# Memory keys copied out of PSUM unscaled and scaled in SBUF, diagonals of 1/rms on ScalarE, later sums of squares, and another branch's gates first

## The chip, the cores and the metric

The kernel runs on one core of one Trainium2 chip. The metric is the time of one execution in microseconds (us), as the median of several runs; smaller is better. In what follows PE is TensorE (the matmul engine), DVE is VectorE, ACT is ScalarE, POOL is GpSimd, and SP is the engine that issues most DMAs.

## What is computed

One step of a one-layer decoder with three parallel branches, for a prompt of 512 tokens and 8 samples of 8 tokens (T = 576 columns in all, 1024 features), with a memory of 256 tokens. Only the part at the program's start and the gates at its end are touched by the change:

```python
def _rmsnorm(x, g):
    y = xf * lax.rsqrt(jnp.mean(xf * xf, axis=-1, keepdims=True) + NORM_EPS)
    return (y * g.astype(jnp.float32)).astype(x.dtype)

def _mem_kv(mem, norm_g, w_kv):
    kv = _rmsnorm(mem, norm_g) @ w_kv           # memory keys and values: outputs, used again later
    mk, mv = jnp.split(kv, 2, axis=-1)

xn = _rmsnorm(x, norm_g)
proj = xn @ w_in                                # one projection that feeds every branch
merged = (sigmoid(m_conv) * (y_conv @ w_branch[0])     # branch 0
          + sigmoid(m_rwkv) * (y_rwkv @ w_branch[1])   # branch 1
          + sigmoid(m_mem)  * (y_mem  @ w_branch[2]))  # branch 2
out = _rmsnorm_final(x + merged @ w_out)
```

## The kernel before

**Number format.** Every operand of a large matmul is split into a high and a low part (`wh` and `wl` of a weight `w`, `mh` and `ml` of the memory, `xh` and `xl` of the normed input), and each product is three matmuls: high by high, high by low, low by high. A weight comes in halves of 128x512 (256 KB each): ACT rounds the half to `wh`, and POOL or DVE subtracts to get `wl` (in the first stage they take turns, half by half).

**Order.** The order on PE is written out by hand. A main generator yields after every few matmuls (one tick), and at each tick every "lane" (a queue of side generators) takes a step; a side generator that yields a number n sleeps for n ticks. So a lag such as `MLAG` sets after how many ticks a side chain's next matmul is put into PE's order. On DVE, ACT, POOL and SP a scheduler decides the order, and each of these engines works its own list strictly from top to bottom: an instruction that waits holds up all that stand behind it.

**The first stage** (`kv`, up to about 68 us) computes memory keys and values:
- Eight key tiles j = 0 to 7 (`w_mk`), each 24 matmuls of 256 columns and 16 ticks. Two tiles share one PSUM buffer `m`, and there are two such buffers, so a tile's buffer must have been read before the second tile pair after it can start.
- Then the values (`w_mv`), 8 steps k of 12 matmuls of 512 columns and 4 ticks each, into two PSUM buffers that are filled alternately, and read at the end into `vst` by ACT.
- The memory is not normed before the product. `mem_rms` computes 1/rms of each memory token beside it (`inv_rms`): ACT squares, DVE adds up to `sq`, PE sums over partitions (line 169, into `z`), DVE makes `ss`, POOL takes the power to `rs`, a diagonal matrix `dg` is made from `rs`, and PE multiplies a matrix of ones by it (line 189), which broadcasts 1/rms over the partitions (`bcs`). `kout` then multiplies each key tile in PSUM by `bcs` on DVE, into `kst`, and every four tiles a DMA on ACT's queue writes `o_mk`.
- The input x (`tr`, four DMAs between key tiles) goes through the same `inv_rms`, in `norm_x`; its broadcast stays in PSUM (`c` and `o`), and for each of 8 feature tiles DVE makes `xn` (two instructions, one per half of the columns), ACT rounds it to `xh` and DVE subtracts to `xl`.
- `mem_rms` and `norm_x` queue one behind the other in the same lane.

**After it** come the projection tiles by `w_in` (48 matmuls of 288 columns each, the first of them is the lora tile), the three branches, and the output product. Weight buffers of this stage are three deep, so the fourth half's `wh` waits until PE has used the first. While PE waits for the rwkv branch's chains, some sigmoid gates are computed ahead (`early_gates`), in the order of `EARLY`, and parked in DRAM; `branch` loads a gate that is there and computes one that isn't. Seven gates get done that way. Branch 2 runs before branch 1, and during branch 1 `wout` prepares the output weights, one step per `lag` ticks.

Of the kernel before, what the change touches and what calls it, by code (L numbers as in the profile page):

```python
# [12 lines left out]
ALU = mybir.AluOpType  # L13
# [8 lines left out]
XS = (2, 3, 5, 6)  # L22
AH = 3
LK = 1
XL2 = 4
MLAG = 51
XLAG = 19


CB = 2  # L30
# [55 lines left out]
def hybrid_step(ctx, tc, x_nat, x_t, mem_t, w_in, w_br, w_mk, w_mv, w_o, kc, vc, swkv,  # L86
# [3 lines left out]
    V, S, G, TE, DMA = (nc.vector, nc.scalar, nc.gpsimd, nc.tensor, nc.sync)  # L90

    def tt(e, out, a, b, op):
        e.tensor_tensor(out=out, in0=a, in1=b, op=op)  # L93
# [4 lines left out]
    def act(out, in_, f=AF.Copy, **k):  # L98
        S.activation(out, in_, f, **k)  # L99
# [22 lines left out]
    def pc(n, j):  # L122
        a = PCOL[n][0] + j
        return par[:, a:a + 1]
# [5 lines left out]
    ident = idt  # L130
# [24 lines left out]
    def inv_rms(tr, ntok, half, pool, ones, lags, out):  # L155
        nt = (ntok + 127) // 128
        sq = pool.tile([128, ntok], F32, name="sq")
        for k in range(8):
            t = pool.tile([128, ntok], F32, name="xn", bufs=2)
            act(sq if k == 0 else t, tr[k], AF.Square)  # L160
            if k:
                tt(V, sq, sq, t, ALU.add)
        yield lags[0]
        z = psd.tile([128, 512], F32, name="s")
        ss = pool.tile([128, nt], F32, name="ss")
        rs = pool.tile([128, nt], F32, name="rs%d" % nt)
        for i in range(nt):
            n = min(128, ntok - i * 128)
            TE.matmul(z[0:n, i:i + 1], sq[:, i * 128:i * 128 + n], ones[:, 0:1], start=True, stop=True)
        nf = ntok // 128  # L170
        for q in (slice(0, nf), slice(nf, nt))[:1 + (nt > nf)]:
            n = 128 if q.start == 0 else ntok - nf * 128
            V.tensor_scalar(ss[0:n, q], z[0:n, q], 1.0 / 1024, 1e-6, op0=ALU.mult, op1=ALU.add)
            tt(G, rs[0:n, q], ss[0:n, q], nhalf[0:n, q], ALU.pow)
        dgs = []
        for i in range(nt):
            n = min(128, ntok - i * 128)
            dg = pool.tile([128, 128], F32, name="dg%d" % i)
            V.tensor_scalar(dg[0:n], ident[0:n], rs[0:n, i:i + 1], None, op0=ALU.mult)
            dgs.append(dg)  # L180
        yield lags[1]
        bc = [pch.tile([128, 512], F32, name=n) for n in "co"[:ntok // half]]
        for i in range(nt):
            n = min(128, ntok - i * 128)
            t0 = i * 128
            while t0 < i * 128 + n:
                h = t0 // half
                t1 = min(i * 128 + n, (h + 1) * half)
                TE.matmul(bc[h][:, t0 - h * half:t1 - h * half], ones[0:n],
                          dgs[i][0:n, t0 - i * 128:t1 - i * 128], start=True, stop=True)  # L190
                t0 = t1
        out += [rs, bc]
# [82 lines left out]
    chain_lane, post_lane, prep_lane, inv_lane, mrg_lane = (Lane() for _ in range(5))  # L275
# [10 lines left out]
    with tc.tile_pool(name="xi", bufs=1) as xi:  # L286
        mtr = xi.tile([128, 8, 256], F32, name="mtr")
        trs = [keep.tile([128, 2, T], F32, name="tr", tag=t) for t in SLOTS]
        tr = [trs[k // 2][:, k % 2, :] for k in range(8)]
        ones = xi.tile([128, 128], F32, name="ones")  # L290
        V.memset(ones, 1.0)
        mh = xi.tile([128, 8, 256], F32R, name="mh")
        ml = xi.tile([128, 8, 256], F32R, name="ml")


        def mem():
            for k in range(8):
                g = pc("norm_mem", k)
                act(mh[:, k, :], mtr[:, k, :], scale=g)
                stt(ml[:, k, :], mtr[:, k, :], g, mh[:, k, :].bitcast(F32), ALU.mult, ALU.subtract)  # L300

        mrs, xrs = [], []
        kst = keep.tile([128, 8, 256], F32, name="kst", tag="s4")
        bcs = xi.tile([128, 256], F32, name="bcs")

        def mem_rms():
            yield from inv_rms([mtr[:, k, :] for k in range(8)], 256, 256, xi, ones, (MLAG, 8), mrs)
            act(bcs, mrs[1][0][:, 0:256])

        def norm_x():  # L310
            yield from inv_rms(tr, T, HT, xi, ones, (XLAG, XL2), xrs)
            for k in range(8):
                xn = xi.tile([128, T], F32, name="xn", bufs=2)
                for h in range(2):
                    stt(v3(xn)[:, h], v3(tr[k])[:, h], pc("norm_in", k), xrs[1][h][:, 0:HT], ALU.mult, ALU.mult)
                act(xh[:, k, :], xn)
                tt(V, xl[:, k, :], xn, xh[:, k, :].bitcast(F32), ALU.subtract)

        def kout(j, ps):
            while not mrs:  # L320
                yield 0
            tt(V, kst[:, j, :], ps[:, j % 2, 0:256], bcs, ALU.mult)
            if j % 4 == 3:
                S.dma_start(out=o_mk[j - 3:j + 1].rearrange("j p m -> p j m"), in_=kst[:, j - 3:j + 1, :])

        def ahead(n):
            if n < 8:
                nxt.append(wload(w_mk[n].rearrange("p k f -> p (k f)"), xi, KBUF))
            elif n < 16:
                nxt.append(wload(w_mv[n - 8], xi, KBUF))  # L330

        nxt = []

        def load_x(j):
            for i in range(4):
                if XS[i] == j:
                    DMA.dma_start(out=trs[i], in_=x_t[:, 2 * i:2 * i + 2])
                    if i == 3:
                        prep_lane.q.append(norm_x())

        def kv():

            z = psd.tile([128, 512], F32, name="s")
            for _ in range(WARM):
                TE.matmul(z[:, 0:128], ones, ones, start=True, stop=True)
            DMA.dma_start(out=mtr[:, 0], in_=mem_t[:, 0])
            ahead(0)
            for a, b in ((1, 2), (2, 4), (4, 6), (6, 8)):
                DMA.dma_start(out=mtr[:, a:b], in_=mem_t[:, a:b])
            DMA.dma_start(out=idt, in_=const_d[:, 0:128])  # L350
            for i in range(1, AH):
                ahead(i)
            mem()
            prep_lane.q.append(mem_rms())
            for j in range(8):
                if j % 2 == 0:
                    ps = pm.tile([128, 2, 512], F32, name="m")
                ahead(j + AH)
                yield from mm(None, mh, ml, 256, ps[:, j % 2:j % 2 + 1], nxt.pop(0))
                post_lane.q.append(kout(j, ps))  # L360
                load_x(j)
            pv = [pm.tile([128, 2, 512], F32, name="m") for _ in range(2)]
            for k in range(8):
                ahead(8 + k + AH)
                load_x(8 + k)
                parts = nxt.pop(0)
                if k == LK:
                    lora_weights(xi)
                    DMA.dma_start(out=con[:, 0:NX], in_=const_d[:, 128:NC1])
                    DMA.dma_start(out=shp, in_=sshift)  # L370
                    DMA.dma_start(out=scv, in_=sconv)
                for q in range(4):
                    t, n = (q // 2, q % 2) if k == 7 else (q % 2, q // 2)
                    h, l = parts[n]
                    ts = slice(t * 128, t * 128 + 128)
                    for i, (a, b) in enumerate(((mh, h), (mh, l), (ml, h))):
                        TE.matmul(pv[t][:, n, :], a[:, k, ts], b,
                                  start=(k == 0 and i == 0), stop=(k == 7 and i == 2))
                    yield
            for t in range(2):  # L380
                st = xi.tile([128, 1024], F32, name="vst")
                act(st.rearrange("p (n f) -> p n f", n=2), pv[t], scale=mrs[0][:, t:t + 1])
                S.dma_start(out=o_mv[t * 128:t * 128 + 128, :], in_=st)
        lo_eng[:] = [G, V]
        drive(kv())
        while prep_lane.busy():
            prep_lane.step()
        lo_eng[:] = [G]


# [9 lines left out]
    def etile(tag, dt=F32, **k):  # L400
        return el.tile([128, T], dt, name="e" + tag, tag=tag, **k)

    EARLY = [(i, j) for i in (1, 2) for j in range(8)]
    gates = {}
    QT = ("r", "k", "A", "B", "C", "D", "E1", "F")
    qt = []
# [9 lines left out]
    with ExitStack() as rctx:  # L416
# [81 lines left out]
        def early_gates():  # L498
            for i, j in EARLY:
                ps = yield from mm(w_in[WM[i] + j])  # L500
# [756 lines left out]
            yield lag  # L1257


    prep_lane.q.append(wout(0, 27))  # L1260
    drive(branch(1, *parts, merged=(mgh, mgl)))
    for _ in wout(1, 0):
        pass
# [8 lines left out]
    for hf in range(2):  # L1272
        h, l = wo[hf]
        for i in range(5):
            n = 128 if i < 4 else 64
# [4 lines left out]
            for q, (c0, c1) in enumerate(((0, 256), (256, 512)) if last else ((0, 512),)):  # L1280
                ps = pm.tile([128, 2, 512], F32, name="m")
# [121 lines left out]
```

## Time and profile before

| | |
|---|---|
| median of 3 runs | 1235.23 us (1234.74 to 1237.84) |
| the profiled execution | 1235.45 us, its span 1233.6 us |
| PE busy | 1186.9 us, 96% of the span |
| DVE, ACT, POOL busy | 48%, 43%, 47% |
| mean granted clock of PE | 0.994 |

PE is the engine that nearly always works, so the time is what PE has to do plus what it waits. Its waits are few: the first 70 us, the rwkv stage from 92 to 630 us, and the last 5 us. A clock of 1.00 is 2.4 GHz, one of 0.50 is 1.2 GHz.

### The profile page before, as it was taken

What the parts mean: (1) busy time and instruction counts of PE and PEld (TensorE: products, weight loads), DVE (VectorE), ACT (ScalarE), POOL (GpSimd) and SP (SyncE); (2) the same over time, 40 slices, a digit from 0 to 9 for tenths busy, and PEclk for the clock granted to TensorE, in tenths of its full rate; (3) what the DMA queues carried; (4) which work ended last, traced back from release to release, by engine and by line L of the source; (5) the groups of instructions that cost most, each with busy time, mean ns of one, the idle gap of its engine ahead of it and who ended that gap; (6) DMA issues with size and microseconds to landing.
All of it is one profiled execution on the core that took longest, in us unless ns stands there. A gap on an engine that the chain in (4) does not pass through costs nothing. (4 is left out here: it accounts for less than half of the span.)

```text
span 1233.6 us, 25594 instructions
## 1 busy us (share of the span) xinstructions
PE 1186.9 (96%) x10158; PEld 1100.8 (89%) x10158; DVE 587.0 (48%) x1514; ACT 524.9 (43%) x1120; POOL 573.8 (47%) x521
## 2 busy tenths in 40 slices
PE   7999979999899999999989999999999999999997
PEld 7798979989798988988879898889899999999976
DVE  7856866468675686647673315213113100134233
ACT  6563446435463544546344435333233222233222
POOL 4535532555535465454543545333334454446642
PEclk9999989999999999999999999999999999999999
DMA  8642222132321322222322225653632222225522
GB/s 290 213 126 72 70 72 63 59 91 58 91 65 53 89 68 84 90 86 70 110 80 74 69 71 171 195 181 123 208 97 87 80 84 86 78 86 161 161 105 78
DMA packets 93056, 129.39 MB, mean 105 GB/s; under 512 B 36988, under 2 KB 41320, under 8 KB 92936
## 3 DMA queue, kind: packets, MB, share of 16 engines
q1 hardware_dynamic: 55888, 110.20, 28.3%
q10 hardware_dynamic: 37048, 17.56, 5.4%
q8 instruction: 80, 1.31, 0.5%
q14 instruction: 40, 0.33, 0.1%
HBM read 115.96 MB, written 11.47 MB: 103 GB/s over the span
## 5 line engine op out<-in xcount | busy, mean ns | idle before, releaser
L93 POOL TENSOR_TENSOR wl<-w,wh 128x512 fp32r<-128x512 f32 x274 | 366.5, 1340 | 490.0 <-ACT wh L99 451.4
L245 PE MATMUL m<-xh,wh 128*128 128x288 f32 x1680 | 370.4, 302 | 0.5 <-ACT vst L99 0.5
L245 PE MATMUL m<-xl,wh 128*128 128x288 f32 x1680 | 369.4, 301 | 0.0
L245 PE MATMUL m<-xh,wl 128*128 128x288 f32 x1680 | 365.2, 299 | 0.0
L99 ACT ACTIVATE wh<-w 128x512 fp32r<-128x512 f32 x290 | 180.5, 627 | 294.2 <-PE m L245 169.1
L245 PEld LDWEIGHTS m<-xh,wh 128*128 128x128 f32 x1680 | 268.8, 189 | 8.6 <-issue 3.7
L245 PEld LDWEIGHTS m<-xl,wh 128*128 128x128 f32 x1680 | 269.2, 189 | 6.4 <-issue 2.9
L245 PEld LDWEIGHTS m<-xh,wl 128*128 128x128 f32 x1680 | 269.4, 189 | 3.0 <-issue 2.1
L96 DVE SCALAR_TENSOR_TENSOR ev<-ev,m 128x576 f32<-128x576 f32 x32 | 24.2, 755 | 168.4 <-PE m L245 110.3
L245 PE MATMUL m<-yh,wh 128*128 128x288 f32 x384 | 82.9, 297 | 0.0
L245 PE MATMUL m<-yh,wl 128*128 128x288 f32 x384 | 82.8, 297 | 0.0
L245 PE MATMUL m<-yl,wh 128*128 128x288 f32 x384 | 82.8, 297 | 0.0
L245 PEld LDWEIGHTS m<-yh,wl 128*128 128x128 f32 x384 | 61.7, 188 | 2.1 <-issue 2.1
L245 PEld LDWEIGHTS m<-yl,wh 128*128 128x128 f32 x384 | 61.7, 188 | 2.1 <-issue 2.1
L245 PEld LDWEIGHTS m<-yh,wh 128*128 128x128 f32 x384 | 61.7, 189 | 2.1 <-issue 2.1
L93 DVE TENSOR_TENSOR c<-c,tmp 108x84 f32<-108x84 f32 (+23 forms) x248 | 56.6, 228 | 5.4
L93 DVE TENSOR_TENSOR tmp<-c,nin 108x84 f32<-108x84 f32 (+23 forms) x248 | 54.8, 221 | 6.7 <-issue 1.2
L96 DVE SCALAR_TENSOR_TENSOR sb<-o,pcl,sb 64x64 f32<-64x64 f32 x112 | 31.6, 282 | 52.1 <-PE o L887 46.0
L99 ACT ACTIVATE osb<-o 64x128 f32<-64x128 f32 x72 | 19.7, 274 | 52.3 <-DVE sb L96 30.5
L93 DVE TENSOR_TENSOR vu<-o,vu 64x128 f32<-64x128 f32 x56 | 15.9, 284 | 46.6 <-PE o L869 45.6
L99 ACT ACTIVATE E<-m,par 128x32 f32<-128x32 f32 (+1 forms) x75 | 27.2, 418 | 22.2 <-PE m L245 14.1
L99 ACT ACTIVATE sb<-sb,pcl 128x128 f32<-128x128 f32 x56 | 22.5, 401 | 29.4 <-DVE sb L96 18.8
(441 smaller groups left out, 1796.2 us busy)
## 6 DMA issues: line engine op xcount, KB each, us to landing
w<-w_in_in SPq DMA_DIRECT2D x210, 256.0 KB
w<-w_br_in SPq DMA_DIRECT2D x48, 256.0 KB
kb<-kc_in SPq DMA_DIRECT2D x16, 512.0 KB
kb<-vc_in SPq DMA_DIRECT2D x16, 512.0 KB
w<-w_mk_in SPq DMA_DIRECT2D x16, 256.0 KB
w<-w_mv_in SPq DMA_DIRECT2D x16, 256.0 KB
w<-w_o_in SPq DMA_DIRECT2D x16, 256.0 KB
nin<-scr ACTq DMA_DIRECT2D x24, 144.0 KB
```

Of the source, the lines that this page charges most:

```text
L93: e.tensor_tensor(out=out, in0=a, in1=b, op=op)
L96: V.scalar_tensor_tensor(out=out, in0=a, scalar=s, in1=b, op0=op0, op1=op1)
L99: S.activation(out, in_, f, **k)
L245: TE.matmul(ps[:, hf, :n], a[:, f], b[:, k, hf * n:hf * n + n], start=(k == 0 and i == 0), stop=(k == 7 and i == 2))
```

## The change

Five edits. `MLAG`, `XLAG` and `XL2` are larger, so the sums of squares and the broadcast of the memory and of x are asked of PE later. The diagonals `dg` are made by ACT instead of DVE. A key tile leaves PSUM as it is, by an ACT copy, and POOL multiplies four tiles at a time by `bcs` in SBUF. `mem_rms` has a lane of its own. And `EARLY` begins with the gates of branch 2 instead of branch 1 (the `lag` of `wout` then depends on how many gates of branch 1 are left; with 9 or more matmul tiles it is 27 as before).

```diff
-XL2 = 4
-MLAG = 51
-XLAG = 19
+XL2 = 5
+MLAG = 90
+XLAG = 42
...
             dg = pool.tile([128, 128], F32, name="dg%d" % i)
-            V.tensor_scalar(dg[0:n], ident[0:n], rs[0:n, i:i + 1], None, op0=ALU.mult)
+            act(dg[0:n], ident[0:n], scale=rs[0:n, i:i + 1])
...
         def mem_rms():
             yield from inv_rms([mtr[:, k, :] for k in range(8)], 256, 256, xi, ones, (MLAG, 8), mrs)
             act(bcs, mrs[1][0][:, 0:256])
+
+            for j in range(0, 8, 4):
+                while kdone[0] < j + 4:
+                    yield 0
+                tt(G, kst[:, j:j + 4, :], kst[:, j:j + 4, :], bcs.unsqueeze(1).to_broadcast([128, 4, 256]), ALU.mult)
+                S.dma_start(out=o_mk[j:j + 4].rearrange("j p m -> p j m"), in_=kst[:, j:j + 4, :])
...
-        def kout(j, ps):
-            while not mrs:
-                yield 0
-            tt(V, kst[:, j, :], ps[:, j % 2, 0:256], bcs, ALU.mult)
-            if j % 4 == 3:
-                S.dma_start(out=o_mk[j - 3:j + 1].rearrange("j p m -> p j m"), in_=kst[:, j - 3:j + 1, :])
...
-            prep_lane.q.append(mem_rms())
+            inv_lane.q.append(mem_rms())
...
                 yield from mm(None, mh, ml, 256, ps[:, j % 2:j % 2 + 1], nxt.pop(0))
-                post_lane.q.append(kout(j, ps))
+                act(kst[:, j, :], ps[:, j % 2, 0:256])
+                kdone[0] = j + 1
...
-    EARLY = [(i, j) for i in (1, 2) for j in range(8)]
+    EARLY = [(i, j) for i in (2, 1) for j in range(8)]
...
-    prep_lane.q.append(wout(0, 27))
+    nt = 16 - sum((1, j) in gates for j in range(8))
+    prep_lane.q.append(wout(0, min(27, (24 * nt - 16) // 8 - 1)))
```

Where the edits move instructions, at three places. First, DVE in the key stage, before the change (the number behind a name tells buffers apart; `ss_340` is the memory's sum of squares, which its 1/rms needs, and `wl_291` belongs to the second half of key tile 5):

```order
L93 TENSOR_TENSOR wl_254<-w_251,wh_253 128x512
L93 TENSOR_TENSOR wl_291<-w_288,wh_290 128x512
L173 TENSOR_SCALAR ss_340<-s_339 128x2
L179 TENSOR_SCALAR dg0_346<-idt_77,rs2_341 128x128
L179 TENSOR_SCALAR dg1_348<-idt_77,rs2_341 128x128
L93 TENSOR_TENSOR sq_505<-sq_505,xn_508 128x576
```

and the same place now (`wl_407` is the second half of value step k = 0, `wl_457` that of step k = 1):

```order
L93 TENSOR_TENSOR wl_255<-w_252,wh_254 128x512
L93 TENSOR_TENSOR wl_293<-w_290,wh_292 128x512
L93 TENSOR_TENSOR wl_331<-w_328,wh_330 128x512
L93 TENSOR_TENSOR wl_370<-w_367,wh_369 128x512
L93 TENSOR_TENSOR wl_407<-w_404,wh_406 128x512
L93 TENSOR_TENSOR wl_457<-w_454,wh_456 128x512
L173 TENSOR_SCALAR ss_429<-s_428 128x2
L93 TENSOR_TENSOR sq_506<-sq_506,xn_509 128x576
```

The memory's `ss` has moved behind four more weight halves; on PE its matmul (line 169) stands after 18 matmuls of key tile 5 instead of 8 of tile 3, and the broadcast (line 189) after 8 matmuls of tile 6.

Second, ACT from there to the last key tile, now (`kst` from `m_360` are key tiles 4 and 5, from `m_447` tiles 6 and 7; `dg0_435` and `dg1_437` are the memory's diagonals; before, no `kst` and no `dg` stood on ACT):

```order
L99 ACTIVATE dg1_437<-idt_77,rs2_430 128x128
L99 ACTIVATE kst_111<-m_360 128x256
L99 ACTIVATE wh_494<-w_492 128x512
L99 ACTIVATE xn_515<-tr_104 128x576
L99 ACTIVATE bcs_112<-c_468 128x256
L99 ACTIVATE wh_500<-w_498 128x512
L99 ACTIVATE xn_518<-tr_105 128x576
L314 DMA o_mk<-kst_111 128x4x256
L99 ACTIVATE kst_111<-m_447 128x256
L99 ACTIVATE xn_521<-tr_105 128x576
L99 ACTIVATE xn_524<-tr_106 128x576
L99 ACTIVATE wh_557<-w_555 128x512
```

Between this and the copy of key tile 7 stand one more `xn`, one more `wh` and the first `lw0`. What moved: eight PSUM copies came to ACT, and the DMA that writes the first four key tiles now waits on ACT's list for POOL's product, ahead of the copies of tiles 6 and 7.

Third, PE at the end of the value product. Before, the sums of squares of x (line 169, `s<-ones,sq`) stood after 15 of the 96 value matmuls and the broadcast after 30, in the middle of them. Now:

```order
L378 MATMUL m<-wh,ml 128x512
L169 MATMUL s<-ones,sq 128x1 x4
L169 MATMUL s<-ones,sq 64x1
L378 MATMUL m<-wh,mh 128x512
...
L378 MATMUL m<-wh,ml 128x512
L189 MATMUL c<-dg_738,ones 128x128
L189 MATMUL c<-dg_740,ones 128x128
L189 MATMUL c<-dg_742,ones 128x32
L189 MATMUL o<-dg_742,ones 128x96
L189 MATMUL o<-dg_744,ones 128x128
L189 MATMUL o<-dg_746,ones 128x64
L245 MATMUL m<-xh,wh 128x288 x2
```

The sums now stand 12 matmuls before the end of the value product, and the broadcast behind all of it, directly ahead of the first projection matmul, which needs `xh`.

And on ACT at that same place, now (`vst_760` and `vst_763` are the two value outputs, `wh_937` is the fourth half of the projection's weights, the first to reuse a buffer):

```order
L99 ACTIVATE dg4_746<-idt_77,rs5_728 64x128
L99 ACTIVATE vst_760<-m_553,rs2_430 128x1024
L384 DMA o_mv<-vst_760 128x1024
L99 ACTIVATE xh_95<-xn_774 128x576
L99 ACTIVATE xh_95<-xn_779 128x576
L99 ACTIVATE vst_763<-m_554,rs2_430 128x1024
L384 DMA o_mv<-vst_763 128x1024
L99 ACTIVATE xh_95<-xn_784 128x576
L99 ACTIVATE xh_95<-xn_789 128x576
L99 ACTIVATE wh_937<-w_935 128x512
L99 ACTIVATE xh_95<-xn_794 128x576
```

The second half of the eight `xh` now stands behind `wh_937`, which waits for PE to be through the first half of the first projection tile. In the rwkv stage PE, DVE and POOL keep their order. In the branches, the matmuls of the seven gates that are loaded fall away in branch 2 and come back in branch 1, the same number.

## Rows read from the trace of the kernel before

**Rows 1.** The page, parts 1 and 2: busy time, share of the span and instructions of PE; then the span in 40 slices of 30.8 us, busy tenths of PE.

```profile
PE 1186.9 (96%) x10158; PEld 1100.8 (89%) x10158; DVE 587.0 (48%) x1514; ACT 524.9 (43%) x1120; POOL 573.8 (47%) x521
PE   7999979999899999999989999999999999999997
```

**Rows 2.** Sums over stretches: from:to, length, busy us (instructions) of PE, weight loads, DVE, ACT and POOL, granted clock, DMA share, GB/s. The rwkv stage, attention with branch 0, the last gates and branches, the output product.

```profile
92.00:630.00 538.00, 510.99 (x5034) 470.26 (x5033) 356.84 (x1067) 259.71 (x597) 269.73 (x262) 0.99 0.27 77
906.00:1172.00 266.00, 266.00 (x1998) 266.00 (x1998) 59.27 (x75) 83.53 (x145) 133.20 (x100) 1.00 0.33 101
```

**Rows 3.** PE's list in order of time where it waited in the first stage: start, duration, operation, shape, count, and in brackets the idle time before it and who ended it.

```profile
20.06 0.61 PE L169 MATMUL s<-ones,sq 128*128 128x1 f32 x4 [0.82 <-DVE sq L93]
24.52 0.71 PE L189 MATMUL c<-dg,ones 128*128 128x128 f32 x4 [2.21 <-DVE dg L179]
26.75 0.35 PE L245 MATMUL m<-mh,wh 128*128 128x256 f32 x1 [1.16 <-DVE kst L93]
32.20 0.36 PE L245 MATMUL m<-mh,wl 128*128 128x256 f32 x1 [0.61 <-DVE kst L93]
39.14 0.36 PE L245 MATMUL m<-mh,wl 128*128 128x256 f32 x1 [0.95 <-DVE kst L93]
69.07 0.53 PE L245 MATMUL m<-xh,wh 128*128 128x288 f32 x2 [0.54 <-ACT vst L99]
```

**Rows 4.** PE's list: the last matmul before the first wait; two key matmuls with 45 between them; the first value matmul; the sums of squares of x.

```profile
18.96 0.28 PE L245 MATMUL m<-ml,wh 128*128 128x256 f32 x1
...
32.40 0.28 PE L245 MATMUL m<-mh,wh 128*128 128x256 f32 x1
...
37.91 0.28 PE L245 MATMUL m<-ml,wh 128*128 128x256 f32 x1
...
41.85 0.40 PE L377 MATMUL m<-wh,mh 128*128 128x512 f32 x1
...
45.37 1.15 PE L169 MATMUL s<-ones,sq 128*128 128x1 f32 x10
```

**Rows 5.** PE's list: the broadcast of x's 1/rms (its first piece and the two before which PE waited), the value matmul behind it, two value matmuls with 62 between them, the second of which is the last of all, and the first pair of the second projection tile.

```profile
49.99 0.38 PE L189 MATMUL c<-dg,ones 128*128 128x128 f32 x2
...
50.84 0.49 PE L189 MATMUL c<-dg,ones 128*128 128x128 f32 x2 [0.47 <-DVE dg L179]
52.06 0.41 PE L189 MATMUL c<-dg,ones 128*128 128x32 f32 x2 [0.73 <-DVE dg L179]
...
53.28 0.50 PE L377 MATMUL m<-wh,mh 128*128 128x512 f32 x1
...
53.85 0.39 PE L377 MATMUL m<-wh,ml 128*128 128x512 f32 x1
...
68.15 0.39 PE L377 MATMUL m<-wh,ml 128*128 128x512 f32 x1
...
75.56 0.42 PE L245 MATMUL m<-xh,wh 128*128 128x288 f32 x2
```

**Rows 6.** Sums over stretches of 2 us after PE's first waits, columns as in rows 2.

```profile
28.00:30.00 2.00, 2.00 (x11) 2.00 (x11) 1.97 (x2) 1.11 (x2) 2.00 (x2) 0.50 1.02 343
30.00:32.00 2.00, 1.60 (x11) 1.39 (x9) 1.75 (x3) 1.77 (x3) 0.83 (x1) 0.82 1.04 391
```

**Rows 7.** SP's list: the issue of the third DMA of x and of the next two weight halves; and the ACT row that waited for that x to land.

```profile
22.58 0.42 SPq L337 DMA_DIRECT2D tr<-x_t_in  x1
23.09 1.65 SPq L224 DMA_DIRECT2D w<-w_mv_in  x2
...
30.23 1.26 ACT L99 ACTIVATE xn<-tr 128x576 f32<-128x576 f32 x2 [0.54 <-DMA tr<-x_t_in]
```

**Rows 8.** ACT's list: a PSUM copy of 128x256, weight rounding, a 64x512 rounding, a 128x128 one.

```profile
25.27 0.39 ACT L99 ACTIVATE bcs<-c 128x256 f32<-128x256 f32 x1 [2.56 <-PE c L189]
35.92 1.20 ACT L99 ACTIVATE wh<-w 128x512 fp32r<-128x512 f32 x2
42.47 0.61 ACT L99 ACTIVATE lw<-lt 64x512 fp32r<-64x512 f32 x1
76.19 0.31 ACT L99 ACTIVATE blkr<-con 128x128 fp32r<-128x128 f32 x1
```

**Rows 9.** POOL's list: the powers of the memory and of x, a weight half, three of them.

```profile
22.45 0.71 POOL L93 TENSOR_TENSOR rs<-ss,nhalf 128x2 f32<-128x2 f32 x1 [1.30 <-DVE ss L173]
23.13 1.26 POOL L93 TENSOR_TENSOR wl<-w,wh 128x512 fp32r<-128x512 f32 x1
46.80 1.53 POOL L93 TENSOR_TENSOR rs<-ss,nhalf 128x4 f32<-128x4 f32 x2 [2.81 <-DVE ss L173]
58.19 4.92 POOL L93 TENSOR_TENSOR wl<-w,wh 128x512 fp32r<-128x512 f32 x3 [0.31 <-ACT wh L99]
```

**Rows 10.** DVE's list: a weight half, the sum of squares, two neighbours of the `xn` pieces (their starts give the pitch), an `xl` alone, and two `xl` beside POOL's work of rows 9.

```profile
12.61 0.68 DVE L93 TENSOR_TENSOR wl<-w,wh 128x512 fp32r<-128x512 f32 x1
46.56 0.22 DVE L173 TENSOR_SCALAR ss<-s 128x4 f32<-128x4 f32 x2 [1.63 <-PE s L169]
58.35 3.61 DVE L93 TENSOR_TENSOR xl<-xn,xh 128x576 fp32r<-128x576 f32 x2
66.80 0.50 DVE L96 SCALAR_TENSOR_TENSOR xn<-tr,par,o 128x288 f32<-128x288 f32 x1
67.22 0.74 DVE L93 TENSOR_TENSOR xl<-xn,xh 128x576 fp32r<-128x576 f32 x1
```

More of the change, by code (lines that the diff above doesn't have):

```diff
@@ L300, in mem @@
                 stt(ml[:, k, :], mtr[:, k, :], g, mh[:, k, :].bitcast(F32), ALU.mult, ALU.subtract)
-        mrs, xrs = [], []
+        mrs, xrs, kdone = [], [], [0]
         kst = keep.tile([128, 8, 256], F32, name="kst", tag="s4")
@@ L385, in hybrid_step @@
         drive(kv())
-        while prep_lane.busy():
+        while prep_lane.busy() or inv_lane.busy():
             prep_lane.step()
+            inv_lane.step()
         lo_eng[:] = [G]
```

## Prediction

> **What bounds the kernel now.** PE is busy for 96% of the span and at nine tenths or more in most slices [rows 1], so a change pays only where PE waits. By stretches: from 906 to 1172 us PE has no idle time at all; from 92 to 630 us it lacks 27 us of 538 [rows 2], but there the change leaves the order as it was. So I read the first 70 us, PE's list first. It waits for the memory's sum (0.82), for its diagonals on DVE (2.21) and three times for a key tile to be scaled out of PSUM by DVE (1.16, 0.61, 0.95) [rows 3]. After the second of these the granted clock is 0.50 and then 0.82 for 2 us each [rows 6], which costs about 1.4 us. The broadcast of x holds up the value product from 49.99 to 53.28, 1.20 of it waiting for DVE's diagonals; the last value matmul ends at 68.4 and the first projection tile at 75.56 [rows 5], after a wait for `vst` of 0.54 [rows 3] and 6.4 us of work. Undisturbed, a key matmul follows the last after 0.12 (46 steps in 5.51) [rows 4], a value matmul after 0.227 (63 steps in 14.30) [rows 5].
>
> **The key stage.** Up to the 80th key matmul (18.96) [rows 4] the change alters little. The memory's sum now stands 58 matmuls on: 19.1 + 7.0 = 26.0. With 0.6 for the sum [rows 3] and 14 matmuls PE is at the broadcast at 28.3. The four waits that DVE caused (2.21, 1.16, 0.61, 0.95) are gone by then: the key tiles leave PSUM by ACT, 0.39 each [rows 8], 3.1 us in all, between work that has seconds of slack.
>
> But when is 1/rms there? DVE has `ss` behind `wl_457`, the second half of value step 1. Its data is the second of the two DMAs issued behind the third x [rows 7]. That x landed at about 30.2 [rows 7], while DMAs moved 343 to 391 GB/s [rows 6]; a half of 256 KB takes 0.7 us at that rate, so the two land at 30.9 and 31.6. Up to there the issues are as before, and the queue is what limits them, so I take these times over. Then ACT rounds (0.6) [rows 8], DVE subtracts (0.68 alone) [rows 10], `ss` takes 0.15, POOL's power 0.71 [rows 9], ACT's two diagonals 0.25 each [rows 8]: 31.6 + 0.6 + 0.7 + 0.15 + 0.7 + 0.5 and a tenth for handing over, 34.4. PE waits 6.1 us for what took 2.21 before. Bounds: 5 if the half lands a microsecond earlier, 7.3 if DVE's and POOL's subtractions meet (two `xl` beside three subtractions of POOL took 3.61, where one alone takes 0.67 by its pitch [rows 9, 10]). At 35.0 the broadcast is done; 40 matmuls take 4.8, and after an idle stretch longer than those before I charge the same 1.4 for a half clock (none to 1.7). The value product starts at 41.2 instead of 41.85: **-0.65**.
>
> **The value product.** ACT's copy of key tile 7 frees the second buffer. ACT's list from the diagonals at 34.4: copy 0.35, round 0.6, square 0.65, `bcs` 0.35 (36.3), and then, two instructions on, the DMA of `o_mk`, which waits for POOL's product of 128x1024. The trace has no such product; by two halves of 128x512 it is 2.5 us [rows 9], from 1.5 (DVE's pace) to 3.5; so from 36.6 after a `wl` to 39.2. Then tile 6's copy, three squares, two roundings, one `lw` [rows 8], about 4.4: the copy of tile 7 is done at 43.9. PE ends the keys at 41.2, does three value matmuls and waits until 43.9: **+2.0** (0 to 3.5). Behind the second `o_mk` the remaining `lw` and four `wh` are late too, but those are needed over 8 us later. The broadcast leaves the value product: **-3.3**. The sums (1.15) [rows 4] stay. The last value matmul ends at 68.4 - 0.65 + 2.0 - 3.3 = 66.45.
>
> The rows put POOL's pace at 1.26 for a half, against 0.68 on DVE [rows 9, 10]; at DVE's pace the product would take 1.4 and the wait would be 0.9 instead of 2.0. The Trainium skill (GPSIMD Engine Reference, Performance versus the Vector engine) speaks against this part of the change: it finds elementwise work with two inputs about twice as slow on GpSimd as on VectorE, and times 2048 columns at 4497 ns. By an estimate from that figure the product of 1024 columns takes 2.25, the wait is 1.7 and the sum 0.3 less than by the rows. The rows, 1.85 times as slow, agree with the page.
>
> **The normed input.** Before, `xh` and `xl` were made beside the value product. Now its 1/rms is asked for 12 matmuls (2.7 us) before the end. `ss` (0.22) [rows 10], the power (1.53 for both parts) [rows 9] and five diagonals on ACT (0.2 each at their pitch) take 2.6, so the broadcast starts without a wait, at 66.45. Without the waits it took 3.29 - 1.20 = 2.1 [rows 5], half for `c`, half for `o`. DVE starts at 0.9 and has 16 pieces of `xn` at a pitch of 0.42 (66.80 to 67.22) and 8 `xl` of 0.67 [rows 10]: 12.1 us. Nothing hides it, since PE's next matmul needs the first `xh` and each further k its own. Two more waits: about 0.4 while ACT rounds the first, and `wh_937`, behind which half of the `xh` stand on ACT: it waits for PE to have used k = 3, whose `xl` DVE gives at 7.5; with 0.8 for PE's six matmuls, 0.6 for `wh_937` and 0.65 for `xh` the fifth `xl` starts at 9.65 instead of 9.2, up to 0.8 later at half clock, and POOL's `wl_938` lies beside it (0 to 1.3). The last `xl` is there at 14.1 to 15.4, and PE needs four more matmuls (0.55): 15.3 in the middle, against 75.56 - 68.4 = 7.15 before: **+8.15**. PE works 6.4 of these 15.3 us, so a clock of 0.50 is likely and would reach into the second tile: **+1.2** (0 to 1.7).
>
> **The other edits.** Gates of branch 2 first: the same seven tiles of 48 matmuls move from branch 2 to branch 1. Loaded gates leave ACT, DVE and POOL 6.4 us for each tile's weights; branch 1 ran that way before without a wait of PE [rows 2]. Were the cover gone at branch 2's start, the last split of its input would cost about 1 us. `wout` keeps its lag of 27. **0.**
>
> **Sum.** -0.65 + 2.0 - 3.3 + 8.15 + 1.2 = +7.4. The profiled execution took 1235.45 with a span of 1233.6, and lies 0.2 above the median of 1235.23; on the median this gives 1242.6.
>
> **Rivals.** A difference under 0.3% (3.7 us) cannot be told from none here.
> - *The forecast*, 1239 to 1247: both waits arise. 0.64; of it 0.06 end within 0.3%.
> - *Only the end of the stage costs.* The half of step 1 lands soon, or DVE's order matters less: the keys end at 28.3 + 0.6 + 4.8 = 33.7, and with no wait the value product ends 23.3 later (21.8 + 1.15 + 0.3), at 57.0. With 15.3 the first tile ends at 72.3, 3.2 earlier; with the clock's 1.2, 2.0 earlier: 1233.2. For it: PE's waits on DVE are really gone. Against it: the x that waited until 30.2. In between, with the wait for 1/rms replaced by one for the copy of tile 7, whose list has a `lora` load ahead of it, about 1237. Together 0.20, within 0.3%; 0.05 of it slower.
> - *The other side, faster.* The wait for 1/rms vanishes altogether: it decides at a landing of the half before about 25.5, when PE doesn't wait at 28.3. Then the value product ends at 57.0, and if the clock stays up through the first projection tile and DVE runs at its floor (0.9 + 12.1 + 0.55 = 13.6), the tile ends at 70.6: 1230.3 to 1232. 0.10, of which 0.02 within 0.3%.
> - *Worse.* POOL's product takes 3.5 and more, and PE stays at half clock through the second projection tile: 1247 to 1251. 0.06.
>
> Faster 0.08, same 0.06 + 0.15 + 0.02 = 0.23, slower the rest, 0.69; I move three hundredths from slower to faster, since the landings rest on one row. The range from 1234.5 to 1247.5 leaves out the faster case and the worse one, some 0.17.
>
> **What would show it.** In the changed trace: PE idle before the memory's line 189 for about 6 us, ended by ACT's `dg`; a wait of about 2 at the fourth value matmul, ended by `kst` on ACT; no wait at line 189 of x; then PE waiting on `xh` and `xl` through the first projection tile, about 9 in all, with a granted clock of 0.50; the second tile about 7 us later than at 75.56; and from 92 us on the same waits, shifted. It is wrong if the value weights land earlier than before, if PE reaches the projection by 60, or if the shift is made up in the rwkv stage, where PE's order and its neighbours' are the same and I see nothing that would.

## The result, and the profile after

The changed kernel takes **1248.68 us** (median of 4 runs, 1246.86 to 1249.81) against 1235.07 (1234.74 to 1237.84) of the kernel before on the same chip: a ratio of 1.0105, with a 95% interval of 1.0089 to 1.0122. It is slower by 13.6 us, where 7.4 was forecast, and lies 1.2 us above the range. The profiled execution took 1249.81, its span 1248.0, with a mean granted clock of 0.987.

The page, parts 1 and 2 (answers [rows 1]): PE's busy time grew by 6.6 us for the same 10158 matmuls, and the second and the third slice lost a tenth each.

```profile
PE 1193.5 (96%) x10158; PEld 1106.0 (89%) x10158; DVE 582.2 (47%) x1499; ACT 529.1 (42%) x1135; POOL 576.1 (46%) x523
PE   7889979999999999999999999999999999999997
```

Sums over stretches, columns as in [rows 2]; the same two stretches as there, each moved by 14.1 us:

```profile
106.10:644.10 538.00, 511.09 (x5036) 470.43 (x5035) 356.35 (x1067) 259.58 (x597) 269.27 (x262) 0.99 0.27 77
920.10:1186.10 266.00, 266.00 (x1998) 266.00 (x1997) 59.94 (x75) 83.96 (x145) 132.14 (x100) 1.00 0.33 103
```

In the rwkv stage PE is busy for 511.09 us now and was for 510.99; the last gates and branches run without idle time as before. So next to nothing is lost or made up from there on: all but 0.3 us of the shift is there at 106 us. PE's list of that stretch, the rows where it waited from the second key tile on and four landmarks (the first and the last value matmul, the broadcast of x that follows at 72.04, and the second projection tile at 88.79); it answers [rows 3] to [rows 5]:

```profile
18.34 0.58 PE L245 MATMUL m<-mh,wh 128*128 128x256 f32 x1 [6.51 <-ACT kst L99]
27.41 0.38 PE L245 MATMUL m<-mh,wh 128*128 128x256 f32 x1 [0.47 <-ACT kst L99]
33.89 0.38 PE L245 MATMUL m<-mh,wh 128*128 128x256 f32 x1 [0.47 <-ACT kst L99]
44.49 0.42 PE L245 MATMUL m<-mh,wh 128*128 128x256 f32 x1 [3.55 <-ACT kst L99]
48.96 0.40 PE L378 MATMUL m<-wh,mh 128*128 128x512 f32 x1
...
71.81 0.39 PE L378 MATMUL m<-wh,ml 128*128 128x512 f32 x1
72.04 0.75 PE L189 MATMUL c<-dg,ones 128*128 128x128 f32 x6
...
75.00 0.53 PE L245 MATMUL m<-xh,wh 128*128 128x288 f32 x2 [1.32 <-ACT xh L99]
75.79 0.85 PE L245 MATMUL m<-xl,wh 128*128 128x288 f32 x2 [0.26 <-DVE xl L93]
81.61 0.53 PE L245 MATMUL m<-xh,wh 128*128 128x288 f32 x2 [1.03 <-ACT xh L99]
83.06 0.53 PE L245 MATMUL m<-xl,wh 128*128 128x288 f32 x2 [0.92 <-DVE xl L93]
84.28 0.53 PE L245 MATMUL m<-xl,wh 128*128 128x288 f32 x2 [0.16 <-DVE xl L93]
85.42 0.66 PE L245 MATMUL m<-xh,wh 128*128 128x288 f32 x2 [0.35 <-ACT xh L99]
88.79 0.56 PE L245 MATMUL m<-xh,wh 128*128 128x288 f32 x2
99.95 0.53 PE L245 MATMUL m<-xh,wl 128*128 128x288 f32 x2 [0.56 <-POOL wl L93]
```

The waits of before are gone (0.82, 2.21, 1.16, 0.61, 0.95 of [rows 3], and one of 0.84 for a `wl` of POOL in the second key tile, at 12.46, that stands in no row there), and others stand in their place. Against the kernel before, the first value matmul starts 7.1 us later (48.96, [rows 4]: 41.85), the last one 3.7 (71.81 to 68.15, [rows 5]), the second projection tile 13.2 (88.79 to 75.56). One more wait of 0.56 for a `wl`, at 99.95, makes it 13.8.

**The first loss: 6.51 us before the second key tile.** The first key tile had ended; the second goes to the other half of the same PSUM buffer, and its first matmul waits for the first tile's copy. In the kernel before, the second tile followed the first without a wait:

```profile
11.22 0.28 PE L245 MATMUL m<-mh,wh 128*128 128x256 f32 x1
```

ACT's list in the changed kernel at that place (columns: start, duration, operation, idle time before it and who ended that):

```profile
15.25 0.42 ACT L99 ACTIVATE xn<-mtr 128x256 f32<-128x256 f32 x1 [0.55 <-DVE sq L93]
15.58 0.61 ACT L99 ACTIVATE wh<-w 128x512 fp32r<-128x512 f32 x1
16.67 0.42 ACT L99 ACTIVATE xn<-mtr 128x256 f32<-128x256 f32 x1 [0.48 <-DVE sq L93]
17.61 0.42 ACT L99 ACTIVATE xn<-mtr 128x256 f32<-128x256 f32 x1 [0.52 <-DVE sq L93]
17.93 0.36 ACT L99 ACTIVATE kst<-m 128x256 f32<-128x256 f32 x1
```

The copy itself takes 0.36. It stands behind the memory's squares (`xn`), of which the later ones wait for DVE's sums (`sq`), since there are two `xn` buffers. PE then works at half clock until 24 us, and again at three places that come up below. Sums over 2 us each, columns as in [rows 6]; in the first stretch PE is idle:

```profile
14.00:16.00 2.00, 0.00 (x0) 0.00 (x0) 1.90 (x2) 1.45 (x4) 2.00 (x2) 0.50 0.75 241
22.00:24.00 2.00, 2.00 (x11) 2.00 (x11) 0.76 (x2) 0.13 (x1) 0.00 (x0) 0.50 0.93 324
46.00:48.00 2.00, 2.00 (x11) 2.00 (x11) 1.90 (x2) 1.59 (x4) 1.57 (x1) 0.50 0.14 42
76.00:78.00 2.00, 2.00 (x9) 2.00 (x10) 2.00 (x5) 1.57 (x2) 0.00 (x0) 0.50 0.05 20
86.00:88.00 2.00, 1.86 (x8) 1.78 (x8) 0.93 (x2) 0.49 (x2) 0.00 (x0) 0.50 0.29 76
```

**The second: 3.55 us before the eighth key tile.** All engines around it, in order of start:

```profile
40.67 2.86 POOL L93 TENSOR_TENSOR kst<-kst,bcs 128x1024 f32<-128x1024 f32 x1
41.26 2.82 DVE L93 TENSOR_TENSOR wl<-w,wh 128x512 fp32r<-128x512 f32 x1
43.56 0.44 ACTq L314 DMA_DIRECT2D o_mk<-kst  x1
44.00 0.74 DVE L93 TENSOR_TENSOR sq<-sq,xn 128x576 f32<-128x576 f32 x1
44.06 0.38 ACT L99 ACTIVATE kst<-m 128x256 f32<-128x256 f32 x1 [2.84 <-POOL kst L93]
```

POOL's product holds the DMA on ACT's list, and the seventh tile's copy stands behind it. Beside it, DVE's subtraction of a half, 0.68 alone [rows 10], lasts 2.82, until the product is over.

**The third: the normed input.** From the last value matmul's end (72.04, where the next matmul starts) to the second projection tile it is 16.75 us now, and was 7.2 before.

### The profile page after: what moved, and what is told of

It reads as the page before. It is cut to its first block, busy times and chain, and to the rows that moved or that the text cites. A ratio compares the mean times of both kernels' runs of the same rounds, so it can differ in the third digit from the quotient of the medians.

```text
span 1248.0 us, 25595 instructions
## 1 busy us (share of the span) xinstructions
PE 1193.5 (96%) x10158; PEld 1106.0 (89%) x10158; DVE 582.2 (47%) x1499; ACT 529.1 (42%) x1135; POOL 576.1 (46%) x523
```

## Experiments

Times are medians. The kernel before was run again beside them: 1235.16 for one copy for two tiles, the later squares, early x and both edits together; 1235.46 for the filled gap, the late products, the diagonals and the version with `MLAG` 51; 1234.70 for the three versions with the products on DVE at the end, and for `EARLY`; 1235.26 for the two with the products on DVE in their place. "Changed" is the changed kernel, 1248.68; its four runs lie between 1246.86 and 1249.81, so against another version of four runs a difference under about 2 us is not clear of the spread.

### The first copy

**One copy for two tiles.**

```diff
-                act(kst[:, j, :], ps[:, j % 2, 0:256])
-                kdone[0] = j + 1
+                if j % 2:
+                    act(kst[:, j - 1:j + 1, :], ps[:, :, 0:256])
+                    kdone[0] = j + 1
```

> The changed kernel with one edit: ACT copies two key tiles at once out of their shared PSUM buffer, after the second of them, instead of each after its own last matmul. Theory A (the second key tile waited 6.51 us because its buffer's first half was to be copied by ACT, and that copy stood behind squares and roundings that wait for DVE): the waits of 6.51, 0.47, 0.47 and 3.55 before odd tiles are gone, the half clock from 14 to 24 us too, and the first value matmul starts at 35 to 38 us instead of 48.96; the end comes 9 to 12 us sooner, at 1236.5 to 1240, since the normed input's chain at the end of the stage stays. Theory B (PE is held by the weights' landings, and the wait only shows where it stood): PE waits as long for wl in the second and third tile, and the time changes by less than 3 us.

Measured: 1238.30, 10.4 less than changed (1.0035 of before, 1.0019 to 1.0050). PE's list has no wait at a key tile from the second on; the first value matmul starts at 35.57. What is left of waits before the value product ends:

```profile
30.17 0.78 PE L189 MATMUL c<-dg,ones 128*128 128x128 f32 x4 [1.25 <-ACT dg L99]
39.59 0.50 PE L379 MATMUL m<-wh,mh 128*128 128x512 f32 x1 [3.16 <-ACT kst L99]
```

Theory A holds and B falls: the weights would have allowed PE to be 13 us earlier at the values. The 3.16 is the wait for the last copy that the forecast had put at the fourth value matmul.

**Squares behind the first copy.**

```diff
-            inv_lane.q.append(mem_rms())
...
+                if j == 0:
+                    inv_lane.q.append(mem_rms())
                 load_x(j)
```

(with `MLAG` 74, which leaves the sum at its place on PE)

> The changed kernel with the memory's squares started after the first key tile (MLAG 74 counted from there, the sum at the same place on PE), so that the copy of the first tile stands ahead of them on ACT; the copies stay one for each tile. Theory A1 (the long wait comes from the copy's place behind the squares): PE waits 0.5 to 1 us at the second tile instead of 6.51, and again about 0.5 before every odd tile; no half clock there; 5 to 9 us sooner than the changed kernel, 1239.5 to 1243.5, if the later 3.55 remains. Theory A2 (the shared buffer alone costs it, whatever stands ahead of the copy): the wait stays above 4 us.

Measured: 1245.09, 3.6 less than changed.

```profile
15.03 0.39 PE L245 MATMUL m<-mh,wh 128*128 128x256 f32 x1 [1.90 <-ACT kst L99]
```

The copy's place on ACT's list was about half of it: the second tile starts 3.3 earlier (15.03 instead of 18.34). The wait fell further, from 6.51 to 1.90, because the first tile, at half clock, ended 1.3 later. The 1.90 that are left are the shared buffer, with the copy still behind two roundings, and 0.47 stands again before the fourth and sixth tile. The gain fell short of the 5 to 9 expected: the clock went to 0.50 here too, once before the wait and once after it, and 3.18 before the eighth tile stayed.

**Work in the gap.** 28 matmuls of ones ahead of the second tile.

> The changed kernel with 28 additional matmuls of ones, which nothing reads, ahead of the second key tile: 6.4 us of work where PE waits 6.51. Theory C (the granted clock of 0.50 from 14 to 24 us follows from the idle time, and cost about 3 us): the second tile starts at about 18.4 as before, the clock stays at 1.00, the second and third tile take 5.8 instead of 9.1 us, and the fourth tile starts near 24.5 instead of 27.41; of these 3 us the end keeps 1 to 3. Rival (the clock falls there for another reason, or something else paces the second and third tile): the fourth tile starts at 27 or later, and the time is within 1 us of the changed kernel.

Measured: 1247.12, 1.6 less than changed, which is not clear of the spread. What the profile shows is clearer. The same two stretches as above, and the fourth tile's start:

```profile
14.00:16.00 2.00, 2.00 (x20) 2.00 (x19) 1.90 (x2) 1.44 (x4) 2.00 (x2) 1.00 0.77 218
22.00:24.00 2.00, 2.00 (x19) 2.00 (x18) 0.97 (x2) 1.03 (x3) 1.16 (x1) 1.00 0.96 324
```

```profile
26.53 0.39 PE L245 MATMUL m<-mh,wh 128*128 128x256 f32 x1 [1.47 <-ACT kst L99]
```

With the gap filled the clock is 1.00 in both stretches, and the second tile takes 2.95 us (19.07 to 22.02) instead of 5.29 (18.34 to 23.63). (From 10 to 12 us, ahead of the filling, it was 0.50 in this profile.) But the fourth tile starts only 0.9 earlier: it waits 1.47 for its partner's copy instead of 0.47. Most of the clock's cost lay beside ACT's list, which came next: ahead of that copy a square of x waits 1.46 there until x has landed.

### POOL's product

**Products and DMAs behind all copies** (asked for 30 ticks after the last key tile).

> The changed kernel with POOL's two products and the two DMAs of o_mk asked for 30 ticks after the last key tile, so that on ACT's list both DMAs stand behind all eight copies. Theory (the 3.55 us before the eighth key tile are the copy of its partner held up by the first DMA, which waits for POOL's product): that wait falls to about 0.5, the half clock from 44.7 to 48.1 goes too, and the first value matmul starts near 44 instead of 48.96; the 6.51 at the second tile stays. If nothing behind it is bound by POOL, 4 to 5 us sooner, 1243.5 to 1244.5. Rival: the products then hold up POOL's weight halves or DVE in the value product, and the wait moves there: less than 2 us.

Measured: 1248.38, nothing gained. PE's list, and ACT's row that ended its idle time there:

```profile
42.76 0.39 PE L245 MATMUL m<-mh,wh 128*128 128x256 f32 x1 [1.41 <-ACT kst L99]
49.99 0.50 PE L379 MATMUL m<-wh,mh 128*128 128x512 f32 x1 [3.39 <-ACT kst L99]
```

```profile
46.30 0.68 ACT L99 ACTIVATE xn<-tr 128x576 f32<-128x576 f32 x1 [3.08 <-DVE sq L93]
```

The wait moved to the value product, as the rival said. The DMA is gone from ACT's list, but POOL's product still ran in the same place (the order of asking only gives a priority), DVE's half beside it took 2.87, the squares of x waited 3.08 for DVE's sums, and the last copy stood behind the squares.

**Products on DVE, in their place.**

```diff
-                tt(G, kst[:, j:j + 4, :], ...
+                tt(V, kst[:, j:j + 4, :], ...
```

> The changed kernel with the key products on DVE instead of POOL and nothing else. If the loss before the eighth tile came through DVE being slowed (its 0.7 us half took 2.8 beside the product): the product takes about 1.2, the half and the sums of squares their own time, and the wait of 3.55 falls to 1 to 1.5 with no new one at the value product; the value product starts at 45 to 46.5 instead of 48.96, and the end comes 2 to 4 us sooner, 1244.5 to 1246.5. If it was the DMA on ACT's list: the copy still waits for the product, 2 us and more, and the time is within 1.5 us of the changed kernel.

Measured: 1244.46, 4.2 less than changed. The wait before the eighth tile and DVE's list there:

```profile
40.82 0.39 PE L245 MATMUL m<-mh,wh 128*128 128x256 f32 x1 [1.43 <-ACT kst L99]
```

```profile
39.70 1.21 DVE L93 TENSOR_TENSOR kst<-kst,bcs 128x1024 f32<-128x1024 f32 x1
40.84 0.68 DVE L93 TENSOR_TENSOR wl<-w,wh 128x512 fp32r<-128x512 f32 x1
```

The product takes 1.21, the half 0.68, and no wait follows at the value product, which starts at 43.80. In this profile 1.5 of the 5.2 us gained by then come from a shorter half clock at the start, so 3.6 are the product's. The two ways in which it reached PE are not separated cleanly: with the product done early, the DMA on ACT's list waits for nothing either. But to take the DMA away alone gained nothing, and to take the product from POOL gained these 3.6.

**Products on DVE behind the last low part of x, both DMAs behind the last `vst`.**

> The changed kernel with the two products moved from POOL to DVE, issued behind the last low part of x, and the two DMAs of o_mk behind the last output of the values. Theory D (POOL's product is what costs the second half of the key stage: while it runs, DVE's work beside it takes three to four times as long, so x's sums and the squares that wait for them are late, and the copies behind those; the DMA on ACT's list was only one way it reached PE): both the 3.55 before the eighth key tile and what came in its place at the value product are below 1 us together, and the value product starts undisturbed near 44.5 to 46; the end comes 3.5 to 5.5 us sooner than the changed kernel, 1243 to 1245. Rival (the squares and sums of x are late by themselves, since x lands at 30 and 33 us): the copy of the last tile is late again, less than 2 us.

Measured: 1246.69, 2.0 less than changed, short of the 3.5 to 5.5 expected and hardly clear of the spread. In the profile, up to the second projection tile (84.70) it gained 4.1, of which 0.9 come from a shorter half clock at the start (the fourth tile starts at 26.54 instead of 27.41); the wait before the eighth tile is 1.43, none stands at the value product, and the values start at 44.47, as theory D said. Then it gave part of this back: 1.61 us of waiting for `er` at 100.21. The cause shows more clearly in the third of the versions below.

### The late x

**`XLAG` 19, `XL2` 4.**

> The changed kernel with XLAG 19 and XL2 4 again, so that the normed input is made beside the value product. If its chain cost 9.6 us at the end (16.75 us from the last value matmul's end to the second projection tile, 7.18 before): the key stage stays as it is, the broadcast costs the value product about 2 us again, and the end comes 6 to 8 us sooner, 1240.5 to 1243. If the chain would have come late anyway because the whole key stage is 7 us late: less than 3 us.

Measured: 1240.63, 8.0 less than changed. The key stage is the same (6.50 and 3.54 stand there again), the value product takes 24.5 us instead of 22.9, the second projection tile starts at 82.16 instead of 88.79. Late x cost 8.0 us by the medians, 6.6 of them by that tile.

**Both: paired copies and early x.**

> Both edits (one copy for two key tiles; XLAG 19 and XL2 4). If the two losses are separate, the gains add up: 9 to 12 and 6 to 8 us less than the changed kernel, 1229 to 1233.5, faster than the kernel before, since the waits of DVE that it had are gone. If the normed input or the value weights bound the stage as soon as the keys are early, the gain of the first edit is lost in the value product: 1234 to 1240.

Measured: **1232.63**, 16.1 less than changed and 0.9982 of before (0.9971 to 0.9993). The gains nearly add up (10.4 + 8.0). What remained:

```profile
38.53 0.50 PE L379 MATMUL m<-wh,mh 128*128 128x512 f32 x1 [3.15 <-ACT kst L99]
43.41 1.75 PE L169 MATMUL s<-ones,sq 128*128 128x1 f32 x10 [1.86 <-DVE sq L93]
```

The values start at 34.53, 7.3 us earlier than before the change, and yet the second projection tile starts at 76.15, where it was 75.56: the keys' lead is lost in these waits, in a half clock from 44 to 51 us, and in DVE's chain for x, which runs from the broadcast (51.24) to 69.4.

### The two other edits

**The diagonals on ACT alone**, on the kernel before.

> The kernel before with one part of the change: the diagonals made by ACT. If DVE's list held them up: the waits of 0.47 and 0.73 in the broadcast of x are gone, the 2.21 before the memory's broadcast falls to about 1.5, and the time to 1232.5 to 1234. If ACT's list holds them up as much: within 0.5 us of the kernel before.

Measured: 1236.76, a ratio of 1.0010 (1.0000 to 1.0020). PE's waits in the key stage:

```profile
24.25 0.49 PE L189 MATMUL c<-dg,ones 128*128 128x128 f32 x2 [1.33 <-ACT dg L99]
27.33 0.58 PE L245 MATMUL m<-mh,wh 128*128 128x256 f32 x1 [1.43 <-DVE kst L93]
40.45 0.36 PE L245 MATMUL m<-mh,wl 128*128 128x256 f32 x1 [1.80 <-DVE kst L93]
```

The waits in x's broadcast went, the 2.21 fell to 1.33 + 0.32, but the waits for `kst` grew (1.16 to 1.43, 0.95 to 1.80), and so did the one for `vst` before the first projection tile (0.54 to 1.57): no gain.

**`EARLY` alone**, on the kernel before.

> The kernel before with one part of the change: the gates of branch 2 computed ahead first. If the cover is the same in both branches, no wait appears in the last branches and the time is that of the kernel before within 1 us; if branch 2's start loses its cover, 1 to 3 us more.

Measured: 1235.04, a ratio of 1.0006 (0.9995 to 1.0017). No effect.

### Versions that were to be faster

**Paired copies, early x, `MLAG` 51**, the products asked for late.

> What is to beat both: the changed kernel with one copy for two key tiles, MLAG 51, XLAG 19 and XL2 4 again, and POOL's products asked for 30 ticks after the last key tile. With the memory's 1/rms at 24 us instead of 29 or later, POOL's first product is done before the copies of the last tiles are due, and the waits of 3.15 (copy) and 1.86 (x's squares, where DVE's sums ran beside POOL's product) that were left are gone: 4 to 7 us less than with the paired copies and the early x alone, 1225.5 to 1228.5. Rival: the product of 2.9 us on POOL slows DVE wherever it stands, and the squares of x are late as often: 1229 to 1233.

Measured: 1234.42 (0.9993 of before, 0.9984 to 1.0002), above both ranges. The waits for the copy and for x's sums went (0.21 is left), but a new one of 2.37 came at x's broadcast, for ACT's diagonals, and the clock fell to 0.50 from 50 to 56 us.

**Paired copies, early x, products on DVE at the end** as above.

> The same products on DVE at the end, with one copy for two key tiles and XLAG 19, XL2 4. Theory D: against the paired copies with early x (1232.6) the waits of 3.15 (copy) and 1.86 (x's sums) and the half clock from 44 to 51 us behind them go, 5 to 8 us: 1225 to 1228. Rival (DVE's chain for x, 17 us from its broadcast on, bounds the stage whatever PE waits for before): the value product only ends with the same wait in the first projection tile, 1229 to 1233.

Measured: 1236.11 (1.0010 of before, 0.9996 to 1.0024), a miss. The second projection tile starts at 73.84, 1.7 us earlier than before the change. Then, ACT's and PE's lists:

```profile
80.22 0.47 ACT L99 ACTIVATE c<-zini 108x352 f32<-108x352 f32 x1 [1.98 <-DMA zini<-const_in]
87.54 0.68 ACT L99 ACTIVATE lx<-eB 64x576 fp32r<-64x576 f32 x1 [2.22 <-DMA eB<-eA]
```

```profile
90.97 0.82 PE L245 MATMUL m<-xh,wh 128*128 128x288 f32 x2 [4.17 <-DVE er L96]
```

The writes of `o_mk` now go out at 72 to 74 us, right before the small transfers on which the lora chain hangs. Those land later (2.22 us of waiting for `eB`, where the kernel before waits 0.44), the chain's next step comes late, and PE waits 4.17. That the writes are what delays them was not tried alone.

**The same with `MLAG` 104.**

> As the last one, with MLAG 104 instead of 90, so that the memory's broadcast stands 21 matmuls later on PE. If the 1.14 before it is only a matter of where it is asked for, it goes, and the time is 0.5 to 1.5 us less than that of the last kernel; if it moves to another wait, the same within 0.5.

Measured: 1235.97. The wait at the memory's broadcast grew (from 0.96 to 2.12) instead of going. `MLAG` moves the sum too: PE makes it at 29.54 instead of 26.50, and the broadcast still comes 14 key matmuls behind it. And POOL's power, which stood at 27.84, now stands behind one more weight half, at 32.22. The rival.

**Paired copies, early x, products on DVE in their place.**

> The version with paired copies and early x (1232.6), with the products on DVE. If DVE's slowing by POOL was behind its two waits (3.15 for the copy, 1.86 for x's sums) and the half clock after them: both together fall below 2 us, and the time to 1227 to 1230.5. If the DMA on ACT's list, or x's landing, sets them: 1231 to 1234.

Measured: 1232.38, 0.9980 of before (0.9970 to 0.9990), inside the second range and no better than with the products on POOL. Waits of 2.50 (copy) and 1.03 (diagonals of x) are left, since here the product on DVE met POOL's weight halves and took 2.21. This and the paired copies with early x are the two versions that beat the kernel before, by 2.9 and 2.5 us.

## Why the prediction was wrong

1. **"Up to the 80th key matmul the change alters little."** This is the step that failed. The second key tile starts at 18.34 instead of 11.22, and what the half clock and the 3.55 add behind it comes to as much as the waits that went: the value product starts 7.1 us late instead of 0.65 early. The copy was costed by its duration (0.39), as work with "seconds of slack", since a buffer was taken to be needed again only by the second tile pair after it. What counted was the copy's place on ACT's list, and that the other half of the same buffer waits for it too: with one copy for both halves 10.4 us came back. [rows 3] had the sign: of the three waits for `kst`, those at 32.20 and 39.14 fall on the third matmul of the sixth and of the eighth tile (by PE's list, 122 and 170 key matmuls stand ahead of them), inside the second tile of a pair, where only its partner's copy can be waited for. The copies of the first tiles caused no such wait there, since they were asked for only after the broadcast, when their partners had been written.
2. **The wait of 6.1 us for 1/rms** didn't arise. PE reached the memory's sum at 36.14 instead of 26.0, and by then nothing was missing. It stays untested: with paired copies PE came at 26.64, but the scheduler had put `ss` ahead of two of the weight halves, and the wait was 1.25.
3. **The product on POOL (+2.0)**: the place on ACT's list and the product's duration (2.5 estimated, 2.86 and 2.40 measured) were right; the wait fell one tile earlier and was 3.55, and the clock of 0.50 from 44.7 to 48 us behind it had not been charged. On DVE the product gave back 4.2. What the term left out is that DVE gets all but nothing done while POOL's product runs: its half takes 2.82 instead of 0.68 and ends 0.55 after the product. The Trainium skill (SBUF — State Buffer, Who interferes with whom) says: "A DVE instruction with two SBUF inputs contends with a GpSimd instruction that reads SBUF", by an exclusive lock on the ports that they share, where the order of issue decides which of them waits. The trace agrees: POOL's product came first (40.67), DVE's half second (41.26). The prediction had cited only the pace of GpSimd.
4. **The broadcast out of the value product (-3.3)** held: from its first to its last matmul 22.85 us instead of 26.30.
5. **The normed input (+8.15, and +1.2 for the clock)** held in size: 16.75 - 7.2 = 9.55. Its inside differed: PE waited 4.0 in six waits instead of 9, and worked at half clock within the first tile (76 to 78 and 86 to 88 us above), where the forecast had the half clock reach into the second. Early x gave 8.0 back.
6. **The other edits (0)** held: the gates of branch 2 first, on their own, changed nothing (1.0006), and the rwkv stage made nothing up. The diagonals on ACT, which belong to the key stage, gained nothing on their own either (1.0010).

At the last value matmul the forecast was 1.95 early and the trace 3.66 late; these 5.6 us, 0.2 more in the normed input and the 0.56 at 99.95 are the whole miss (6.4 against 6.2). The time lies in the rival "worse" (1247 to 1251), but by another mechanism: neither a product of 3.5 nor a half clock through the whole second tile. The half clock, item by item, is not summed up here: filling the first gap showed that its cost partly lies beside other waits.

## What to carry to other kernels

Cost a read out of PSUM by where it stands on its engine's list and by every matmul that waits for its buffer, the other half included, not by its duration. Before a two-input product goes to GpSimd, ask what VectorE does meanwhile: here its own two-input work lost nearly the whole time of the product. Work that is moved behind the last matmuls that hid it is on the path with its whole length, and where a wait is taken away, the next one on the same list is to be looked for before the gain is counted.

## What was not expected of the hardware

- VectorE's two-input operations beside GpSimd's product took about four times as long: a half 2.82 instead of 0.68, a sum of squares 2.95 instead of 0.76 (paired copies with early x, at 32.84).
- Near the start PE's clock can be at 0.50 without a long gap ahead of it. With the paired copies it was, with waits of 0.58 and 0.44 before it, and in the kernel before, with the same waits, it was not; the two rows are from the paired copies' and from the earlier kernel's profile:

```profile
10.00:12.00 2.00, 2.00 (x12) 2.00 (x11) 1.35 (x4) 2.00 (x6) 0.43 (x1) 0.50 1.05 404
```

```profile
10.00:12.00 2.00, 1.62 (x13) 1.41 (x11) 1.44 (x4) 2.00 (x6) 0.88 (x1) 1.00 1.05 404
```

  The first key tile took 1.4 us longer there, so a difference of that size between two single profiles proves nothing about an edit.
